# Output projection of a two-layer mixer: the place of the fourth products, one written order for two blocks, and two gate weights

## The chip, the cores and the metric

The kernel runs on one core of a Trainium2 chip. A core has a matrix engine (TensorE, PE in the profile, with its weight loads as PEld), a vector engine (DVE), a scalar engine (ACT), a general engine (GpSimd, POOL) and a queue for transfers (SyncE, SP). Matmuls write into banks of PSUM, 128 x 512 fp32 each; DVE and ACT read them from there. Operands lie in SBUF. The metric is the device time of one execution in microseconds; lower is better.

## The reference

Two layers over 1024 latent tokens and 256 context tokens, model width 1024. The even layer has a convolution branch and a recurrent branch, each with a SiLU gate, then one output projection. The odd layer is a multi-scale pooling mixer. Cut to what this change touches:

```python
# even layer: the recurrent branch's gate
y_b = y_b * silu(gb)                     # gb = h @ w_in[:, last quarter]
out = concat([y_a, y_b]) @ w_out
# odd layer
z = h @ p["w_in"]                        # 1024 -> 4096
u, g = split(z)                          # 2048 each
y = einsum(multiscale_pool(u), w_grp) * scale
out = (y * silu(g)) @ p["w_out"]         # 2048 -> 1024
x = x + gate * out
return rmsnorm(x, final_g)
```

The change lies in the product with the odd layer's `w_out` (the output projection below), and, in its last part, in the gate `silu(gb)` of the even layer.

## The kernel before, in words

Everything is kept transposed: a tile has 128 channels as partitions and the 1024 tokens along the free axis, in two halves of 512. Every fp32 factor is split into a high part (a cast to fp32r on ACT) and a low part (a subtraction on DVE or POOL), and each matmul runs as three: high by high, high by low, low by high.

**The output projection.** The contraction over 2048 channels is done in two halves of 1024: part 0 (tiles 0 to 7 of y) and part 1 (tiles 8 to 15). Part 0's result is scaled by the gate, added to the residual and written back to memory; part 1 adds to that and goes on to the final norm. Each part runs over four blocks, m = 0, 2, 4, 6, of two output tiles by two token halves. A block is a two by two matrix product in Winograd's form with seven block products in place of eight. On the side of y the seven operands are called b11, t1, t2, b21, t3, b22, t4 (`BOPS`); on the side of the weights they are numbered: 1 goes with b11, 5 with t1, 6 with t2, 2 with b21, 7 with t3, 3 with b22, 4 with t4. "The fourth product" is that of weight 4 and t4. `prod` (line 1148) issues one of them: four k steps of three matmuls into one bank.

A block uses three PSUM banks out of a pool of four: qa takes b11 and, after ACT has copied it to qb, b21; qc takes t1 and b22; qb, which starts from the copy, takes t2, t3 and t4. After a product has finished an output quarter, or half of it, `put` takes it out. In part 0 the half results of t1 and t2 are copied by ACT (`keep_part`, line 1205, tiles s_wo), because their banks are filled again; that of t3 is copied too (`copied`, line 1826, tile b_wo). The finished quarter is then put into a residual tile xp by DVE (`gated`, line 1819), which SP has loaded from `x1_part` (line 1883) and stores back (line 1892). Two kinds of xp tiles take turns, so a load waits for the store of two uses before.

**Orders.** Most of the kernel is ordered by a scheduler that simulates it when the kernel is built; `tc.issue_after(i)` (and `held`) puts what is traced inside behind instruction i on i's engine. `linked` (line 1835) chains the products of part 0 on PE, so their order is the written one; in part 1 `quad` (line 1163) leaves the order to the scheduler. In part 0 the order of a block is b11, [t4 of the block before], t1, t2, b21, b22, t3 (in the first block t3 before b22); `quad_linked` returns the block's own t4 as a function `last`, which the next block calls as `pend`. The last one, t4 of block 6, is handed to the first block of part 1. From block 4 of part 1 on, `last_half0` does the first token half alone, and the rest is in a written order of its own.

**Weights.** `wo1_weights` loads two raw tiles for a block (`wr`, two buffers, line 1116), forms the sums and splits seven operands (`wquad_steps`, line 1112): weight 1, then the difference for 7, the sum for 5, and so on; 4 is the last. Seven tiles out of a ring of eight take the results, so a split can wait for a product of the block before.

**Operands of y.** The seven operands per part have been stored to memory (`y_raw`) and are loaded back by `y_operand` (line 1691), 512 KB at a time, two loads each, then split by ACT and DVE. With `later` the splits are put off. For t3, b22 and t4 of part 0 this happens after the last gate's SiLU; for part 1 in the `ahead` of its first block, t3 first, then b22 and t4, whose raw data is loaded into their own low tiles (no raw tile). `x2_load` (line 1910) loads two residual tiles for part 1.

**The gates of the recurrent branch** (lines 1217 to 1245). For j = 3 to 8 the loop takes, in a fixed order on each engine: the raw weight of product j + 2 (`gb_weights`: cast on ACT, subtraction on POOL, tiles wh_gb, wl_gb; from j = 6 on the first weights of the output projection, wh_wob, wl_wob), the two SiLUs of product j (`gb_silu`, tiles sb from a ring of four), the product j + 2 on PE, and then `gated(j - 1)`: load of a recurrent row yr, multiplication on DVE, cast on ACT (ybh), subtraction on POOL (ybl), with `fill` steps of the convolution on DVE in between. The product wob then reads ybh and ybl.

Of the kernel before, what the change touches and what calls it, by code (L numbers as in the profile page):

```python
# [16 lines left out]
S = 1024  # L17
# [3 lines left out]
KT = D // P  # L21
# [30 lines left out]
def body(ctx, tc, xT, ctxT, cc, ccol, modT, modW, win, gw, wout, wu, grp, wg, wo1, small, edge, ident, outT):  # L52
    nc = tc.nc
# [55 lines left out]
    class Written:  # L109

        def __init__(self, eng):
            self.eng, self.last = eng, None
# [1050 lines left out]
    def quad(w, name, ops, put, ahead=None, tied=False, mid=None, pend=None):  # L1163
        p1, p2, p3, p4, p5, p6, p7 = w
        a, c, b = psum(f"qa_{name}"), psum(f"qc_{name}"), psum(f"qb_{name}")
        if pend is None:
            prod(a, p1, ops["b11"], True, False)
        else:
            pend[0](a, p1, ops["b11"], True, False)
        with tc.high_priority(offset=EVAC):  # L1170
            evac = nc.scalar.copy(b, a)
        if pend is not None:
            pend[1]()
        if mid is not None:
            with tc.issue_after(evac.ins):
                mid()
        prod(c, p5, ops["t1"], True, False)
        with tc.high_priority(offset=EVAC):
            put(1, 1, c, 0)
        prod(b, p6, ops["t2"], False, False)  # L1180
        with tc.high_priority(offset=EVAC):
            put(0, 1, b, 0)
        prod(a, p2, ops["b21"], False, True)
        with tc.high_priority(offset=EVAC):
            put(0, 0, a, None)
        w = None
        if ahead is not None:
            with tc.issue_after(evac.ins):
                w = ahead()
        mm = prod(b, p7, ops["t3"], False, False)  # L1190
        with tc.high_priority(offset=EVAC):
            put(1, 1, b, 1)
        with tc.issue_after(mm.ins) if tied else nullcontext():
            prod(c, p3, ops["b22"], False, True)
        with tc.high_priority(offset=EVAC):
# [37 lines left out]
    gb_product(5, gws[5])  # L1233
    gated(1, 3)
    for j in range(3, KT + 1):
        if 3 < j < KT - 1:
            gb_weights(j + 2)
        if j < KT:
            gb_silu(j)
        if 3 < j < KT - 2:  # L1240
            gb_product(j + 2, gws[j + 2])
        gated(j - 1, (0, 0, 4, 5, 5, 3, 1, 0)[j - 1])
        if j == KT:
            gb_weights(KT + 1)
            fill(8)
        ln_sums()
# [444 lines left out]
    def y_operand(ops, part, name, raw_tile, alloc, later=None, hold=None):  # L1691
        hi, lo = [], []
        for q in range(2):
            if raw_tile is None:
                lo.append(alloc(f"y{part}_{name}l{q}", F32R))
                r = lo[q].bitcast(F32)
            else:
                r = raw_tile(f"yr_{part}_{name}_{q}")
            nc.sync.dma_start(r, y_raw[part][name][:, q * S : (q + 1) * S])
# [11 lines left out]
    yops = [{}, {}]  # L1711

    def y_operands(part, raws, names=BOPS, alloc=None, later=None, hold=None):
        for name in names:
# [19 lines left out]
    for m in range(0, NK, 2):  # L1734
# [63 lines left out]
        w = quad(wq, f"g{m}", bx, to_gate, first_out if m == NK - 2 else None)  # L1798
        if m == NK - 2:
            with tc.issue_after(silu[0].ins):  # L1800
                y_operands(0, iter([xtile] * 7), BOPS[4:])
        for i in range(2):
            for h in range(2):
                gt = rows(ys[m + i][:, HALF[h]])
# [30 lines left out]
    def linked(*args):  # L1835
        with held(chain[0]):
            chain[0] = prod(*args)

    def quad_linked(w, name, ops, put, ahead, order, pend):
        p1, p2, p3, p4, p5, p6, p7 = w  # L1840
        a, c, b = psum(f"qa_{name}"), psum(f"qc_{name}"), psum(f"qb_{name}")
        linked(a, p1, ops["b11"], True, False)
        with tc.high_priority(offset=EVAC):
            evac = nc.scalar.copy(b, a)
        if pend is not None:
            pend()
        linked(c, p5, ops["t1"], True, False)
        with tc.high_priority(offset=EVAC):
            put(1, 1, c, 0)
        linked(b, p6, ops["t2"], False, False)  # L1850
        with tc.high_priority(offset=EVAC):
            put(0, 1, b, 0)
        linked(a, p2, ops["b21"], False, True)
        with tc.high_priority(offset=EVAC):
            put(0, 0, a, None)
        with tc.issue_after(evac.ins):
            nxt_ = ahead()
        for name in order:
            if name == "t3":
                linked(b, p7, ops["t3"], False, False)  # L1860
                with tc.high_priority(offset=EVAC):
                    put(1, 1, b, 1)
            else:
                linked(c, p3, ops["b22"], False, True)
                with tc.high_priority(offset=EVAC):
                    put(0, 1, c, 1)

        def last():
            linked(b, p4, ops["t4"], False, True)
            with tc.high_priority(offset=EVAC):  # L1870
                put(1, 0, b, None)
        return nxt_, last

    last_ = None
    for m in range(0, KT, 2):

        def put(i, h, x, part, m=m, parts={}):
            if part == 0:
                keep_part(parts, f"wo0_{m}", i, x)
                return  # L1880
            xp_n[0] += 1
            t = (vtile, lambda name: atile(name)[:, :H])[xp_n[0] % 2](f"xp{m}_{i}_{h}")
            nc.sync.dma_start(t, x1_part[m + i][:, HALF[h]])
            if part == 1:

                if i == 1:
                    x = copied(f"wo0_{m}", x)
                s = x if i == 0 else parts[i]
                nc.vector.tensor_tensor(out=s, in0=x, in1=parts[i], op=add)
                x = s  # L1890
            gated(m + i, t, x)
            nc.sync.dma_start(x1_part[m + i][:, HALF[h]], t)
            if (m, i, h, part) == (2, 1, 1, 1):
                y_sums(NK - 2)
        def nxt(m=m):
            if m < KT - 2:
                with tc.issue_after(stored[0].ins):
                    return wo1_weights(0, m + 2)
            w = wo1_weights(1, 0)
            y_operands(1, iter([xtile]), BOPS[3:4])  # L1900
            return w

        if m == KT - 2:
            with tc.issue_after(loaded[0].ins):
                y_operands(1, iter([xtile] * 2), BOPS[1:3])
        w, last_ = quad_linked(w, f"wo0_{m}", yops[0], put, nxt, ("b22", "t3") if m else ("t3", "b22"), last_)
        if m == 2:
            with tc.issue_after(loaded[0].ins):
                y_operands(1, iter([xtile]), BOPS[:1], lambda name, dt: xtile(name, dt), hold=copied_[0])
# [4 lines left out]
                nc.sync.dma_start(x1[k], x1_part[k])  # L1914

    x2_load(0)
    for m in range(0, KT - 4, 2):
# [7 lines left out]
        def ahead():  # L1925
            if m == 0:
                y_operands(1, iter([xtile, None, None]), BOPS[4:])
            w = wo1_weights(1, m + 2)
            x2_load(m + 2)
            return w  # L1930

        w = quad(w, f"wo1_{m}", yops[1], put, ahead, pend=None if m else (linked, last_))


    ops = yops[1]
# [21 lines left out]
    def last_half0(m, w, ahead=None):  # L1957
# [3 lines left out]
        prod(a, p1, ops["b11"], True, False)  # L1961
        with tc.high_priority(offset=EVAC):
            evac = nc.scalar.copy(b, a)
        mm = prod(d, p4, ops["t4"], True, True)
        with tc.high_priority(offset=EVAC):
            gated(m + 1, y0, d)
        nxt = None
        if ahead is not None:
            with tc.issue_after(evac.ins):
# [16 lines left out]

    m = KT - 4
    wa = w
    wb, _, _ = last_half0(m, wa, ahead)
    _, tail["pe"], tail["dve"] = last_half0(m + 2, wb)  # L1990


# [218 lines left out]
```

## Time and profile before

| | |
|---|---|
| median of three runs | 1275.95 us (1275.37 to 1275.96) |
| the profiled execution's own time | 1272.99 us |
| its span | 1271.2 us, 16213 instructions |
| PE busy | 1252.5 us (99%), 5858 matmuls |
| PEld, DVE, ACT, POOL busy | 1034.5, 1141.8, 654.9, 291.8 us |
| mean granted TensorE clock | 0.996 |
| read, written | 137.18 MB, 44.04 MB, 143 GB/s over the span |
| gates of the recurrent branch | about 440 to 500 us |
| part 0 of the output projection | from 1093.7 us |
| part 1, first block | from about 1173 us |

A row of the time line has the start in us from the span's start, the duration in us, the engine, the line of the code, the operation, out<-in by tile names, the shapes, how many such instructions stand together, and in brackets how long the engine sat idle before it and what ended that. Matmuls overlap: each is shown with 0.39 us, and a new one starts every 0.23 us, so a stall of PE is longer than the idle time that the row shows. A row of waits has the waiting engine, tile and line, what it waited for, then us in total, how often, and the longest. A row of stretches gives the busy time of each engine in that stretch with the number of instructions.

### The profile page before, as it was taken

To read this page: it belongs to the slowest core of one execution; us is meant where nothing else is said; L and a number is where in the kernel's file an instruction comes from. 1 tells how busy PE (TensorE), PEld (TensorE's weight loads), DVE (VectorE), ACT (ScalarE), POOL (GpSimd) and SP (SyncE) were. 2 spreads that over 40 slices of the span, in tenths; PEclk is the share of its full clock that TensorE was granted. 3 is DMA by queue.
4 is the path that set the end of the run, shared out by engine and by line. 5 is a ranking of instruction groups with operands and counts; after the bars stand their busy time and mean duration, and the time that the engine had idled before them with its cause. 6 is when DMAs were issued, how large, how long until landed. Compare 5 with 4: busy or idle time off the path is not lost. (4 is left out here: it accounts for less than half of the span.)

```text
span 1271.2 us, 16213 instructions
## 1 busy us (share of the span) xinstructions
PE 1252.5 (99%) x5858; PEld 1034.5 (81%) x5858; DVE 1141.8 (90%) x1748; ACT 654.9 (52%) x955; POOL 291.8 (23%) x176
## 2 busy tenths in 40 slices
PE   9999999999999999999999999999999999999996
PEld 7788888888888887888887788788888888778785
DVE  7799999999999999988978979999999977877876
ACT  8464566556656533137435446644444344735542
POOL 0015364536453556433210022000000000000003
PEclk9999999999999999999999999999999999999998
DMA  9970111112111234442526665344432334868723
GB/s 378 387 251 28 58 59 67 42 53 64 62 63 59 77 114 133 158 140 84 172 91 226 207 216 160 105 151 141 135 122 83 125 116 156 299 198 271 283 69 133
DMA packets 78705, 182.29 MB, mean 143 GB/s; under 512 B 7712, under 2 KB 23328, under 8 KB 78624
## 3 DMA queue, kind: packets, MB, share of 16 engines
q1 hardware_dynamic: 69632, 176.53, 40.7%
q10 hardware_dynamic: 8992, 4.72, 1.3%
q8 instruction: 46, 0.75, 0.3%
q14 instruction: 35, 0.29, 0.1%
HBM read 137.18 MB, written 44.04 MB: 143 GB/s over the span
## 5 line engine op out<-in xcount | busy, mean ns | idle before, releaser
L670 DVE SCALAR_TENSOR_TENSOR conv<-u,sm,conv 128x505 f32<-128x505 f32 (+6 forms) x224 | 153.7, 744 | 1.0
L1943 POOL TENSOR_TENSOR o<-x,rr 128x256 f32<-128x256 f32 (+1 forms) x10 | 9.7, 1009 | 453.4 <-ACT rr L1943 453.4
L670 ACT ACTIVATE l<-g,sm 128x512 f32<-128x512 f32 (+1 forms) x96 | 58.7, 619 | 57.7 <-PE g L670 57.0
L670 POOL TENSOR_TENSOR l<-l,l 128x1280 f32<-128x1280 f32 x16 | 47.1, 2965 | 25.6 <-ACT l L670 15.1
L670 PE MATMUL wob<-ybl,wh_wob 128*128 128x512 f32 x128 | 49.9, 390 | 1.1 <-POOL ybl L670 1.1
L670 PE MATMUL va<-h0h,wl_va 128*128 128x512 f32 x128 | 49.9, 390 | 0.2 <-DVE wl_va L670 0.2
L670 PE MATMUL wob<-ybh,wl_wob 128*128 128x512 f32 x128 | 49.9, 390 | 0.1
L670 PE MATMUL gb<-h0l,wh_gb 128*128 128x512 f32 x128 | 49.8, 389 | 0.0
L670 PE MATMUL gb<-h0h,wh_gb 128*128 128x512 f32 x128 | 49.8, 389 | 0.0
L670 PE MATMUL va<-h0l,wh_va 128*128 128x512 f32 x128 | 49.8, 389 | 0.0
L670 PE MATMUL wob<-ybh,wh_wob 128*128 128x512 f32 x128 | 49.8, 389 | 0.0
L670 PE MATMUL va<-h0h,wh_va 128*128 128x512 f32 x128 | 49.8, 389 | 0.0
L670 PE MATMUL gb<-h0h,wl_gb 128*128 128x512 f32 x128 | 49.8, 389 | 0.0
L670 DVE TENSOR_TENSOR_SCAN l<-l,l 128x256 f32<-128x256 f32 (+1 forms) x32 | 48.7, 1522 | 1.1
L98 ACT CAST wq_wo<-wr_wo 128x512 fp32r<-128x512 f32 x48 | 28.9, 620 | 40.1 <-DMA wr_wo<-wo 17.8
L670 DVE SCALAR_TENSOR_TENSOR conv<-cL,wsum,conv 128x506 f32<-128x506 f32 (+3 forms) x70 | 48.1, 744 | 0.2
L670 POOL TENSOR_TENSOR l<-l,uc 128x1280 f32<-128x1280 f32 x16 | 47.7, 3005 | 0.0
L98 ACT CAST wq_g<-wr_g 128x512 fp32r<-128x512 f32 x48 | 28.3, 621 | 33.5 <-DVE wr_g L1133 12.6
L670 PE MATMUL xb<-h0l,wh_xb 128*128 128x512 f32 x112 | 43.8, 391 | 0.0
L670 PE MATMUL xb<-h0h,wh_xb 128*128 128x512 f32 x112 | 43.8, 391 | 0.0
L670 PE MATMUL xb<-h0h,wl_xb 128*128 128x512 f32 x112 | 43.6, 389 | 0.0
L670 PE MATMUL vg<-h0h,wh_vg 128*128 128x512 f32 x112 | 43.6, 389 | 0.0
(624 smaller groups left out, 4320.1 us busy)
## 6 DMA issues: line engine op xcount, KB each, us to landing
modw<-modW SPq DMA_DIRECT2D x16, 512.0 KB, 10.2
x_part<-xp SPq DMA_DIRECT2D x32, 256.0 KB, 2.9
mod<-modT SPq DMA_DIRECT2D x32, 256.0 KB, 3.5
wr_v<-wfold SPq DMA_DIRECT2D x16, 512.0 KB, 3.6
wr_g<-wg SPq DMA_DIRECT2D x16, 512.0 KB, 4.9
wr_wo<-wo SPq DMA_DIRECT2D x16, 512.0 KB, 4.6
mod<-modT SPq DMA_DIRECT2D x14, 512.0 KB, 4.5
yr_t<-y_t SPq DMA_DIRECT2D x14, 512.0 KB, 7.3
```

The lines of the kernel that those rows point to most:

```text
L98: return (nc.scalar.copy(hi, src), eng.tensor_tensor(out=lo, in0=src, in1=hi.bitcast(F32), op=sub))
L670: last[eng] = f(*args, **kw)
L1943: tail[eng] = f(*args, **kw)
```

## The change

Five edits. (1) In `quad`, the pending product comes after t1, not before; no caller hands it one any more after the change. (2) In the gate loop, `gb_weights(j + 2)` for j = 5 and 6 stands behind `gb_silu(j)`. (3) The splits of b22 and t4 of part 0 are put off until after the copy of the first block's t2 (`kept_`). (4) In `quad_linked`, `pend` comes after t1 and its put. (5) The first two blocks of part 1 are written out in one order with a small class, `Quad`, chained on PE; the loads of b22 come before those of t4, and x of block 2 behind t4's; block 2's own t4 runs in `last_half0` of block 4.

```diff
@@ quad
-        if pend is not None:
-            pend[1]()
...
-        prod(c, p5, ops["t1"], True, False)
+        if pend is None:
+            prod(c, p5, ops["t1"], True, False)
+        else:
+            pend[0](c, p5, ops["t1"], True, False)
+            pend[1]()
@@ gates
     for j in range(3, KT + 1):
-        if 3 < j < KT - 1:
+        if j == 4:
             gb_weights(j + 2)
         if j < KT:
             gb_silu(j)
+        if 4 < j < KT - 1:
+            gb_weights(j + 2)
@@ y_operand
-            nc.sync.dma_start(r, y_raw[part][name][:, q * S : (q + 1) * S])
+            d = nc.sync.dma_start(r, y_raw[part][name][:, q * S : (q + 1) * S])
+            if name in ("b22", "t4"):
+                y_loaded[name == "t4"] = d
@@ last gate block
             with tc.issue_after(silu[0].ins):
-                y_operands(0, iter([xtile] * 7), BOPS[4:])
+                y_operands(0, iter([xtile]), BOPS[4:5])
+                y_late = []
+                y_operands(0, iter([xtile] * 2), BOPS[5:], later=y_late)
@@ quad_linked
-        if pend is not None:
-            pend()
         linked(c, p5, ops["t1"], True, False)
         with tc.high_priority(offset=EVAC):
             put(1, 1, c, 0)
+        if pend is not None:
+            pend()
@@ part 0, weights of the next block
         def nxt(m=m):
+            if m == 0:
+                with tc.issue_after(kept_[0].ins):
+                    for v in y_late:
+                        split(*v, nc.vector)
@@ part 1, blocks 0 and 2
-        w = quad(w, f"wo1_{m}", yops[1], put, ahead, pend=None if m else (linked, last_))
...
+    class Quad:
...
+        def run(self, op):
+            n, p, first, last, args = dict(
+                b11=("a", 1, True, False, None), t1=("c", 5, True, False, (1, 1, 0)),
+                t2=("b", 6, False, False, (0, 1, 0)), b21=("a", 2, False, True, (0, 0, None)),
+                t3=("b", 7, False, False, (1, 1, 1)), b22=("c", 3, False, True, (0, 1, 1)),
+                t4=("b", 4, False, True, (1, 0, None)))[op]
+            linked(self.bank(n), self.w[p], yops[1][op], first, last)
+            if args is not None:
+                i, h, part = args
+                with tc.high_priority(offset=EVAC):
+                    self.put(i, h, self.bank(n), part)
...
+    q0.run("b11")
+    q0.copy()
+    q0.run("t1")
+    last_()
+    q0.run("t2")
+    q0.run("b21")
+    with tc.issue_after(q0.evac.ins):
+        late_ = []
+        y_operands(1, iter([None]), BOPS[5:6])
+        y_operands(1, iter([xtile]), BOPS[4:5])
+        with held(y_loaded[0]):
+            y_operands(1, iter([None]), BOPS[6:], later=late_)
+        w = wo1_weights(1, 2)
+        for v in late_:
+            split(*v, nc.vector)
+        with held(y_loaded[1]):
+            x2_load(2)
+    q2 = Quad(w, "wo1_2", wo1_put(2))
+    q2.run("b11")
+    q0.run("t3")
+    q0.run("b22")
+    q2.run("t1")
+    q2.copy()
+    q0.run("t4")
+    q2.run("t2")
+    q2.run("b21")
+    with tc.issue_after(q2.evac.ins):
+        w = wo1_weights(1, 4)
+        x2_load(4)
+    q2.run("b22")
+    q2.run("t3")
@@ last_half0 (block 4 of part 1)
-        mm = prod(d, p4, ops["t4"], True, True)
+        if pend is None:
+            mm = prod(d, p4, ops["t4"], True, True)
+        else:
+            mm = linked(d, p4, ops["t4"], True, True)
...
+        if pend is not None:
+            pend("t4")
```

More of the change, by code (lines that the diff above doesn't have):

```diff
@@ L1837, in linked @@
             chain[0] = prod(*args)
+        return chain[0]
     def quad_linked(w, name, ops, put, ahead, order, pend):
@@ L1916, in body, with wo1_put @@
     x2_load(0)
-    for m in range(0, KT - 4, 2):
+    def wo1_put(m):
         def put(i, h, x, part):
@@ L1924, in put, with __init__, bank, copy @@
                 square_fin(m + i, h, slice(0, H), v)
[L1925 to L1930, printed above, removed]
-        w = quad(w, f"wo1_{m}", yops[1], put, ahead, pend=None if m else (linked, last_))
+        return put
+    class Quad:
+        def __init__(self, w, name, put):
+            self.w, self.name, self.put = dict(zip(range(1, 8), w)), name, put
+            self.ps = {}
+        def bank(self, n):
+            if n not in self.ps:
+                self.ps[n] = psum(f"q{n}_{self.name}")
+            return self.ps[n]
+        def run(self, op):
[9 more added lines that the diff above has]
+                    self.put(i, h, self.bank(n), part)
+        def copy(self):
+            with tc.high_priority(offset=EVAC):
+                self.evac = nc.scalar.copy(self.bank("b"), self.bank("a"))
@@ new lines, in body @@
+    q0 = Quad(w, "wo1_0", wo1_put(0))
+    for n in "acb":
+        q0.bank(n)
+    q0.run("b11")
[15 more added lines that the diff above has]
+            x2_load(2)
@@ L1955, in fin_add, with last_half0 @@
         return nc.vector.tensor_tensor(out=acc_, in0=acc_, in1=q, op=add)
-    def last_half0(m, w, ahead=None):
+    def last_half0(m, w, ahead=None, pend=None):
         p1, p2, p3, p4, p5, p6, p7 = w
@@ L1960, in last_half0 @@
         (x0, x1_), (y0, y1) = [[x1[m + i][:, h] for h in HALF] for i in range(2)]
-        prod(a, p1, ops["b11"], True, False)
+        with held(chain[0] if pend is not None else None):
+            prod(a, p1, ops["b11"], True, False)
         with tc.high_priority(offset=EVAC):
             evac = nc.scalar.copy(b, a)
-        mm = prod(d, p4, ops["t4"], True, True)
+        if pend is None:
+            mm = prod(d, p4, ops["t4"], True, True)
+        else:
+            mm = linked(d, p4, ops["t4"], True, True)
         with tc.high_priority(offset=EVAC):
             gated(m + 1, y0, d)
+        if pend is not None:
+            pend("t4")
         nxt = None
@@ L1988, in body, with last_weights @@
     wa = w
-    wb, _, _ = last_half0(m, wa, ahead)
+    def last_weights():
+        w = wo1_weights(1, KT - 2)
+        x2_load(KT - 2)
+        return w
+    wb, _, _ = last_half0(m, wa, last_weights, q2.run)
     _, tail["pe"], tail["dve"] = last_half0(m + 2, wb)
```

2 lines of the change are left out of this document (1 added, 1 removed).

## The prediction

> **What bounds the kernel now.** I read the page first, then the stretches of 40 us of the output projection, then the waits of TensorE.
>
> ```profile
> 1100.00:1140.00 40.00, 37.92 (x166) 30.76 (x165) 31.89 (x46) 20.08 (x32) 0.00 (x0) 1.00 0.67 220
> 1140.00:1180.00 40.00, 38.72 (x169) 31.14 (x168) 32.65 (x47) 19.57 (x31) 0.00 (x0) 1.00 0.82 278
> 1180.00:1220.00 40.00, 38.84 (x169) 31.40 (x169) 31.64 (x45) 22.65 (x35) 0.00 (x0) 1.00 0.57 202
> ```
>
> ```profile
> PE qb_wo L1152 <- ACT b_wo L1828: 2.2, 2, 1.3
> PE qb_wo L1152 <- ACT s_wo L1207: 1.2, 1, 1.2
> ```
>
> The columns of the stretches are busy us of PE, PEld, DVE, ACT and POOL, then granted clock, DMA share and GB/s. PE is busy for 115.5 of the 120 us, at clock 1.00: this stage is bound by the matmuls, and all that any new order can win is the 4.5 us between them and a little at their restarts. These two rows head the waits of PE in the whole kernel: it waits for ACT to copy a bank (b_wo, s_wo).
>
> **Unit of the sums.** Twelve matmuls make a product, and the starts below give their pitch (1108.95 to 1109.18): 0.23 us, so a product is 2.72 us. I call the pairs of column tiles block 0, 2, 4, 6, and write t4(2) for the product on operand t4 of block 2. A stall is start minus previous start minus 0.23, and each restart loses 0.11 more on its second matmul (1108.61 to 1108.95).
>
> **Part 1: two operands of the first half are split later.** PE stops at t3(0):
>
> ```profile
> 1107.04 0.39 PE L1155 MATMUL qa_wo<-y_b21h,wq_wo 128*128 128x512 f32 x1
> 1108.61 0.50 PE L1152 MATMUL qb_wo<-y_t3h,wq_wo 128*128 128x512 f32 x1 [1.19 <-ACT s_wo L1207]
> 1108.95 0.39 PE L1154 MATMUL qb_wo<-y_t3l,wq_wo 128*128 128x512 f32 x1
> 1109.18 0.39 PE L1155 MATMUL qb_wo<-y_t3h,wq_wo 128*128 128x512 f32 x1
> ```
>
> ```profile
> 1106.08 1.05 ACT L98 CAST y_t4h<-yr_t 128x1024 fp32r<-128x1024 f32 x1 [1.75 <-DMA yr_t<-y_t]
> 1107.03 1.04 ACT L98 CAST y_b22h<-yr_b 128x1024 fp32r<-128x1024 f32 x1
> 1107.98 0.58 ACT L1207 COPY s_wo<-qb_wo 128x512 f32<-128x512 f32 x1
> ```
>
> The bank qb is full after t2(0), but its copy s_wo stands on ACT behind a cast of t4 that waits for its DMA, and behind a cast of b22. The change puts the four casts of b22 and t4 behind that copy; they run on ACT and DVE while t3(0) runs (2.72 us; the first b22 cast and its subtraction take 1.05 and 1.22). No load is added, and none moves. Worth: 1.34 + 0.11 = **1.45 us**. If that cover is gone, b22(0) waits instead, at most the 1.45 again.
>
> **Part 2: t4 of a block runs after the next block's b11 and t1**, no longer between them. The two stalls meant are these:
>
> ```profile
> 1135.72 0.39 PE L1155 MATMUL qa_wo<-y_b11h,wq_wo 128*128 128x512 f32 x1
> 1137.01 0.50 PE L1152 MATMUL qb_wo<-y_t4h,wq_wo 128*128 128x512 f32 x1 [0.90 <-ACT b_wo L1828]
> ...
> 1175.55 0.39 PE L1155 MATMUL qa_wo<-y_b11h,wq_wo 128*128 128x512 f32 x1
> 1177.21 0.50 PE L1152 MATMUL qb_wo<-y_t4h,wq_wo 128*128 128x512 f32 x1 [1.27 <-ACT b_wo L1828]
> ```
>
> They cost 1.06 + 0.11 and 1.43 + 0.11. A product more in between covers both. But t1 now comes 2.72 us earlier, and what it needs is late too: its weight (fifth of seven, split on ACT and DVE after the block's second raw tile has landed) and its bank qc, which the block before gives back when DVE has put it into the residual. The rows for blocks 2, 4 and 6:
>
> ```profile
> 1117.85 0.74 DVE L1820 SCALAR_TENSOR_TENSOR xp<-qc_wo,m,xp 128x512 f32<-128x512 f32 x1
> ...
> 1138.80 0.68 DVE L99 TENSOR_TENSOR wq_wo<-wr_wo,wq_wo 128x512 fp32r<-128x512 f32 x1
> ...
> 1158.51 0.74 DVE L1820 SCALAR_TENSOR_TENSOR xp<-qc_wo,m,xp 128x512 f32<-128x512 f32 x1
> ...
> 1159.31 0.19 PEld L1152 LDWEIGHTS qc_wo<-y_t1h,wq_wo 128*128 128x128 f32 x1 [0.42 <-DVE xp L1820]
> ```
>
> Without any stall t3(0) starts at 1107.27, and t1(2), t1(4), t1(6) follow after 3, 10 and 17 products: at 1115.4, 1134.5 and 1153.5. By the rows of before, bank or weight stand ready at 1118.6, 1139.0 (the low half, which the third matmul reads, ends at 1139.5) and 1159.3. The lateness is 3.2, 4.6 and 5.8 us; a wait at an earlier one covers the later, so the largest counts: w is between 0 and 5.8 if nothing is ready later than before. What makes them ready follows PE's events in part (the bank is full 1.45 earlier after part 1; the second raw tile is loaded when the block before has split its last weight, which waits for t2), and in part the DMAs. I take the middle, w = 2.9. Before, t1(6) starts at 1159.31 with t4(4) done; after, at 1153.5 + w with t4(4) still to come, so the same work is reached at 1156.2 + w: -3.1 + 2.9 = **-0.2 us** for part 1 and the blocks 2 to 6 of part 2 together (their stalls at 1108.61 and 1137.01 are in it). The stall at 1177.21 comes on top, with t1 of the second half's block 0 (weights and x tiles without a write-back) in no such need: **-1.5 us**.
>
> The wait that is added lies with the loads, too: the t4 evacuation is every fourth use of the xp tiles, and each xp load waits for the store of two uses before; t4's store is now 2.72 later, and SP's queue (weight loads among it) stands behind.
>
> ```profile
> wr_wo<-wo SPq DMA_DIRECT2D x11, 512.0 KB, 5.7
> ```
>
> The raw weights take 5.7 us at the median of this stage. [...]
>
> **Part 3: second half, blocks 0 and 2 in one written order.** Before, SP has the second load of b22 behind two loads of x, which wait for tiles that the split of t3 gives back:
>
> ```profile
> 1182.44 0.54 SPq L1699 DMA_DIRECT2D y_b22l<-y_b  x1
> 1190.25 2.11 SPq L1914 DMA_DIRECT2D x<-x_part  x2
> 1192.41 0.42 SPq L1699 DMA_DIRECT2D y_b22l<-y_b  x1
> ```
>
> ```profile
> 1193.62 0.39 PE L1155 MATMUL qb_wo<-y_t3h,wq_wo 128*128 128x512 f32 x1
> 1194.66 0.50 PE L1152 MATMUL qc_wo<-y_b22h,wq_wo 128*128 128x512 f32 x1 [0.65 <-ACT y_b22h L98]
> 1195.67 0.50 PE L1152 MATMUL qb_wo<-y_t2h,wq_wo 128*128 128x512 f32 x1 [0.51 <-ACT qb_wo L1171]
> ```
>
> PE loses 0.81 + 0.78 + 0.11 there. After, b22's loads come first, x after t4's, and every bank rests two products (5.4 us) between its uses. I take all of it: **-1.7 us**; bounds 0 to -1.8. The x loads now stand behind t4's; block 2 first needs them after nine products, 24.5 us after the half's start (1173.1, one product before the end of 1175.55 + 0.23). Issued as now, until 1192.4, they have 5 us to land; if that cover goes, evacuations wait, and PE only after the two products of rest.
>
> **Part 4: two gate weights behind their gates.** PE waits at the stage after the recurrence for POOL's low half of the last rows:
>
> ```profile
> 494.96 0.50 PE L670 MATMUL wob<-ybl,wh_wob 128*128 128x512 f32 x1 [1.11 <-POOL ybl L670]
> ```
>
> ```profile
> 473.00 1.30 POOL L670 TENSOR_TENSOR ybl<-sb,ybh 128x512 fp32r<-128x512 f32 x1 [3.04 <-ACT ybh L670]
> 474.27 2.41 POOL L670 TENSOR_TENSOR wl_gb<-wr_gb,wh_gb 128x1024 fp32r<-128x1024 f32 x1
> ...
> 484.29 2.40 POOL L670 TENSOR_TENSOR wl_wob<-wr_wob,wh_wob 128x1024 fp32r<-128x1024 f32 x1
> ```
>
> ```profile
> 475.44 2.39 DVE L670 TENSOR_TENSOR lnsum<-lnsum,u 128x512 f32<-128x512 f32 x2
> ...
> 485.63 1.60 DVE L670 TENSOR_TENSOR sb<-yr,sb 128x512 f32<-128x512 f32 x1
> ```
>
> ```profile
> 492.00 0.60 ACT L670 ACTIVATE sb<-gb 128x512 f32<-128x512 f32 x1 [0.91 <-POOL ybl L670]
> ```
>
> All four engines have a fixed order here. The two DVE rows are long because POOL's subtraction of a weight runs: lnsum ends 0.55 after 476.68, and so with the other (usual is 0.68). A gate's second SiLU waits for POOL's ybl (the last row), so the cast behind it comes 2.1 us later than before and POOL's weight starts at about 476.0 and 487.2 instead of 474.27 and 484.29. At the first place DVE meets it between two sums and comes out 1.1 later; at the second its multiply is already through and 0.9 is won back. Net at ybl: **+0.3**, bounds -0.9 and +1.5.
>
> **Sum.** -0.2 - 1.5 - 1.7 + 0.3 = -3.1 us. The profiled execution took 1272.99 us (its span 1271.2), 2.96 under the median 1275.95 of the three runs; -3.1 on that median is 1272.8.
>
> **The rivals.** (A) *The same waits at another product*: the t1 products find bank and weight no earlier than before, w = 5.8 or a little over: -0.2 in all, 1275.8. For it: the row at 1159.31 already waits for the bank. Against: three of the releases follow PE.
> (B) *Slower: the write-back ring.* From t4's end to the bank's return the round behind block 4 took 19.4 us (t4(2) starts at 1137.01 and takes 2.83; the put into the residual ends at 1159.25), and the new order leaves five products, 13.6 us, to the next t1 of that bank. If that round keeps its length, t1(6) is late by 5.8, and if the other two (to t1(4) and to t1 of the next half) and t1(2) are late by half as much, 2.9, 2.9 and 1.6, the waits are 13.2 in all in place of 2.9, the sum is +7.2 and the time 1283.2. It decides from waits of 8.6 in all. Against: ACT, DVE and SP's queue serve raw weights in the same round, so part of its length is queueing that a new order may lose.
> (C) *The written order starves block 2*: if SP sends its raw weights behind the loads of y that now come first, by one landing (5.7 us) more than they have to spare, b11(2) of the second half stops for that: +2.6, 1278.6, slower by a hair. Before, SP did send them first, though they are traced behind y.
> (D) No effect of the first half's t4 move alone, if the scheduler moves DVE's order with it: w = 0, -6.0, 1270.0.
>
> **How the numbers follow.** Two executions of this kernel differ by up to 0.6 us, and 0.2% (2.6 us) is what I call a change. Likeliest, with D in it: 0.47, its own range 1269.5 to 1273.4. A: 0.24. B: 0.20. C: 0.09. So faster 0.47, same 0.24, slower 0.29. The range goes from w = 0 with a gain in part 4 (1269.0) to where B has four fifths of its lateness (1280.5).
>
> **What would show it.** Part 1: s_wo ahead of the casts of b22, no stall at t3(0). Part 2: no PE wait for b_wo; at t1 of blocks 2, 4, 6 waits for xp or for a weight, 2.9 in sum (over 6: A; over 9: B). Part 3: both b22 loads ahead of x, no wait in the first two blocks. Part 4: POOL's two weights at 476 and 487, the stall at ybl 1.3 to 2. A span above 1273.8 makes the forecast wrong.

## The result, and the profile after

The changed kernel takes 1276.75 us (median of 22 runs, 1274.08 to 1278.48), the kernel before beside it 1274.81 us (22 runs, 1272.85 to 1278.65). The ratio is 1.0015, with a 95% interval of 1.0008 to 1.0022: about 1.9 us slower, where 3.1 us faster was forecast. The profiled execution has a span of 1273.5 us (before 1271.2). The 1275.95 from which the forecast counted was the median of three runs, 1.1 us above that of 22.

All stalls of PE, added up as in the prediction (start minus previous start minus 0.23, where that is over 0.03), by stage and kernel, in us:

| stage | before | after |
|---|---|---|
| start, to 60 us | 2.86 | 3.55 |
| gates, 440 to 520 | 1.76 | 0.72 |
| 660 to 820 | 2.84 | 2.87 |
| part 0 of the output projection, to 1172, and t4(6) | 4.65 | 6.51 |
| part 1, blocks 0 and 2, 1182 to 1202 | 1.86 | 2.43 |
| tail, from 1222 | 2.41 | 2.42 |
| 60 to 140 and 820 to 960 | 0.87 | 0.88 |
| whole span | 17.26 | 19.38 |

The start is not touched by the change and lies between 2.8 and 3.9 in the profiles of this study, so the 0.7 there is chance. The rest: the gates win 1.0, part 0 loses 1.9, part 1 loses 0.6.

PE's waits in the changed kernel, in the same columns as before (waiter, releaser, us, times, longest):

```profile
PE qc_wo L1152 <- DVE xp L1828: 2.8, 2, 1.8
PE qa_wo L1155 <- DVE wq_wo L99: 1.9, 2, 1.2
```

The waits for ACT's copies s_wo and b_wo are gone, as meant. In their place PE waits for the bank qc and for a low half of weights. The time line of PE shows where:

```profile
1114.46 0.50 PE L1155 MATMUL qa_wo<-y_b11h,wq_wo 128*128 128x512 f32 x1 [1.25 <-DVE wq_wo L99]
1118.88 0.47 PE L1152 MATMUL qc_wo<-y_t1h,wq_wo 128*128 128x512 f32 x1 [1.82 <-DVE xp L1828]
...
1120.33 0.63 PE L1155 MATMUL qc_wo<-y_t1h,wq_wo 128*128 128x512 f32 x1
1120.76 0.63 PE L1152 MATMUL qc_wo<-y_t1h,wq_wo 128*128 128x512 f32 x1
...
1122.89 0.63 PE L1155 MATMUL qc_wo<-y_t1h,wq_wo 128*128 128x512 f32 x1
...
1159.91 0.47 PE L1152 MATMUL qc_wo<-y_t1h,wq_wo 128*128 128x512 f32 x1 [0.95 <-DVE xp L1828]
```

b11(2) stops for 1.42 us, t1(2) for 1.99, t1(6) for 1.11 (each by the formula above, a little more than the idle time in the bracket). Between 1120.33 and 1122.89 the matmuls come every 0.43 us in place of 0.23, with no wait shown. The stretches of the same kernel say why (busy us of PE, PEld, DVE, ACT, POOL, then granted clock, DMA share, GB/s):

```profile
1116.60:1120.01 3.41, 1.59 (x7) 0.85 (x7) 3.41 (x7) 1.71 (x3) 0.00 (x0) 1.00 0.33 124
1120.01:1123.42 3.41, 3.41 (x10) 2.63 (x9) 1.22 (x2) 0.00 (x0) 0.00 (x0) 0.50 0.58 183
1123.42:1126.84 3.42, 3.42 (x17) 2.83 (x16) 1.23 (x2) 1.11 (x2) 0.00 (x0) 1.00 0.25 30
```

For 3.41 us TensorE ran at half clock (0.50), which costs 1.7 us. The pause ahead of it lies in the stretch before.

In part 1 both loads of b22 now go out ahead of x of block 2, but each of t3's raw tiles (yr_t) goes out behind one of t4's:

```profile
1179.40 0.72 SPq L1703 DMA_DIRECT2D y_b22l<-y_b  x1
1180.16 0.90 SPq L1703 DMA_DIRECT2D y_t4l<-y_t  x1
1182.31 0.32 SPq L1703 DMA_DIRECT2D yr_t<-y_t  x1
1183.51 0.32 SPq L1703 DMA_DIRECT2D y_t4l<-y_t  x1
1184.47 0.32 SPq L1703 DMA_DIRECT2D yr_t<-y_t  x1
```

Before, both of t3's loads were issued from 1178.18 on (row yr_t x2). On ACT the second cast of b22 waits for its data ahead of the casts of block 2's first weights, and b11 of block 2 waits for these, as PE's rows under ACT's show:

```profile
1188.87 1.05 ACT L98 CAST y_b22h<-y_b22l 128x1024 fp32r<-128x1024 f32 x1 [4.30 <-DMA y_b22l<-y_b]
1189.83 1.13 ACT L98 CAST wq_wo<-wr_wo 128x512 fp32r<-128x512 f32 x2
```

PE, same kernel:

```profile
1190.49 0.50 PE L1152 MATMUL qa_wo<-y_b11h,wq_wo 128*128 128x512 f32 x1 [0.38 <-ACT wq_wo L98]
1191.84 0.50 PE L1155 MATMUL qa_wo<-y_b11h,wq_wo 128*128 128x512 f32 x1 [0.61 <-DVE wq_wo L99]
```

These stops of b11(2), 1.52 us with their restarts, come with the later fourth products and not with the written order, as `e3` and `e6` below show.

In the gates POOL's two weights start at 476.90 and 486.02, and no matmul of wob waits any more; one product gb waits 0.60 us for the first of them.

### The profile page after: what moved, and what is told of

Its sections match the earlier page's. It is cut to its first block, busy times and chain, and to the rows that moved or that the text cites. A ratio compares the mean times of both kernels' runs of the same rounds, so it can differ in the third digit from the quotient of the medians.

```text
span 1273.5 us, 16213 instructions
## 1 busy us (share of the span) xinstructions
PE 1254.7 (99%) x5858; PEld 1036.0 (81%) x5858; DVE 1139.2 (89%) x1748; ACT 655.9 (51%) x955; POOL 295.0 (23%) x176
## 5 line engine op out<-in xcount | busy, mean ns | idle before, releaser
L670 PE MATMUL vg<-h0l,wh_vg 128*128 128x512 f32 x112 | 43.6, 389 | 0.0
```

Source lines behind the costliest of these rows:

```text
L670: last[eng] = f(*args, **kw)
```

## The experiments

Every ratio is against the kernel before, run on the same chip beside it, with its 95% interval.

### Each part of the change alone

`e1_gates` has the gate loop's hunk, `e2_splits` the late splits, `e3_t4` the later fourth products, `e4_order` the written order of part 1 (with `last_` before t1, as before). The core of each:

```diff
# e1
-        if 3 < j < KT - 1:
+        if j == 4:
             gb_weights(j + 2)
...
+        if 4 < j < KT - 1:
+            gb_weights(j + 2)
# e2
-                y_operands(0, iter([xtile] * 7), BOPS[4:])
+                y_operands(0, iter([xtile]), BOPS[4:5])
+                y_late = []
+                y_operands(0, iter([xtile] * 2), BOPS[5:], later=y_late)
# e3, in quad_linked, and the like in quad
-        if pend is not None:
-            pend()
         linked(c, p5, ops["t1"], True, False)
...
+        if pend is not None:
+            pend()
# e4
-        w = quad(w, f"wo1_{m}", yops[1], put, ahead, pend=None if m else (linked, last_))
+    q0 = Quad(w, "wo1_0", wo1_put(0))
...
+    q0.copy()
+    last_()
+    q0.run("t1")
```

> The kernel before with the gate weights' new place alone. Theory from the trace after: the stall of wob for ybl goes (1.38 and 0.39 us) and one of 0.4 for the gate weight comes, so about 1.1 us faster than before (ratio 0.9991). The prediction: +0.3 us, a stall of 1.3 to 2 for ybl stays.

> The kernel before with the late splits of b22 and t4 alone. Theory: the stall at t3(0) goes (-1.45 us), but weight 1 of block 2 stands on ACT and DVE behind the four splits, so b11(2) waits about 1.5 us: 0 in all. Rival (the prediction): -1.45 us and no new wait. A third: b11(2) waits longer than t3(0) did, slower by up to 1 us.

> The kernel before with the later place of the fourth products alone (first half, and the first block of the second). [...] Rival B: the write-back ring is slower, t1 waits of over 9 us in sum, +7. The prediction's middle: -0.2 - 1.5 without part 1's 1.45, about -0.3.

> The kernel before with the written order of the first two blocks of the second half alone, t4 of the last block of the first half before t1 as before. Theory from the trace after: waits of b11 of block 2 for its weights (0.65 and 0.89 us) and of t3 (0.48 and 0.42) in place of 1.87: +0.6 us. Rival (the prediction): -1.7 us with no wait. Rival C: one landing later, +2.6.

| kernel | median us | ratio | interval |
|---|---|---|---|
| e1, gates | 1274.52 | 1.0000 | 0.9991 to 1.0009 |
| e2, late splits | 1270.73 | 0.9965 | 0.9953 to 0.9978 |
| e3, t4 later | 1276.01 | 1.0009 | 1.0000 to 1.0017 |
| e4, written order | 1281.34 | 1.0053 | 1.0039 to 1.0067 |
| before | 1274.62 | | |

The theories for `e2` and `e4` missed by far; `e3` is 0.09% slower, about 1.2 us, where the prediction's middle was 0.3 us faster. The late splits win 0.35%, three times what their stall is worth; the written order loses 0.53%; the gates alone can't be told from no change, and their forecast of 0.9991 stands at the edge of the interval. The sum of the four is +0.27%, the whole change +0.15%, so the parts do not simply add.

In `e2` the stall at t3(0) is gone and b11(2) stops for 1.43 in its place, as the theory had it. PE's row on the time line of `e2`:

```profile
1115.17 0.50 PE L1155 MATMUL qa_wo<-y_b11h,wq_wo 128*128 128x512 f32 x1 [1.27 <-DVE wq_wo L99]
```

DVE's rows ahead of it in the same kernel:

```profile
1112.68 0.69 DVE L1132 TENSOR_TENSOR ws_wo<-wr_wo,wr_wo 128x512 f32<-128x512 f32 x1 [1.44 <-DMA wr_wo<-wo]
1113.30 1.22 DVE L99 TENSOR_TENSOR y_t4l<-yr_t,y_t4h 128x1024 fp32r<-128x1024 f32 x1
1114.43 0.69 DVE L99 TENSOR_TENSOR wq_wo<-wr_wo,wq_wo 128x512 fp32r<-128x512 f32 x1
```

Weight 1 of block 2 stands behind a moved subtraction of t4. What `e2` wins lies later: at t4(2) (1.16 before, 0; but t1(4) and the start of part 0 lose 0.97 more), at t4(6) (1.54 before, 0) and in blocks 0 and 2 of part 1 (1.86 before, 0.23). Nothing of that is in the edit. Its SP queue tells a good part of it. In the kernel before, the raw weights of block 6 were sent at 1145.49, behind the load of a residual tile:

```profile
1145.08 0.32 SPq L1883 DMA_DIRECT2D xp<-x_part  x1
1145.49 0.86 SPq L1116 DMA_DIRECT2D wr_wo<-wo  x2
```

In `e2` they go ahead of it, 3.3 us earlier:

```profile
1142.18 2.07 SPq L1116 DMA_DIRECT2D wr_wo<-wo  x2
1144.30 0.42 SPq L1885 DMA_DIRECT2D xp<-x_part  x1
```

The scheduler, with the splits later, had exchanged the two.

In `e3` the two products t1 wait for the bank, 1.83 and 2.04 us, at 1119.79 and 1160.23: 1.4 us more than the waits for b_wo had cost (1.06 and 1.43), at another product. And b11(2) of part 1 stops, 1.08 us with its restarts, though `e3` has no written order. On ACT a cast of t4 that waits for its data stands ahead of the weights' casts:

```profile
1188.11 1.05 ACT L98 CAST y_t4h<-y_t4l 128x1024 fp32r<-128x1024 f32 x1 [7.97 <-DMA y_t4l<-y_t]
1189.07 1.13 ACT L98 CAST wq_wo<-wr_wo 128x512 fp32r<-128x512 f32 x2
```

PE in `e3`:

```profile
1191.68 0.50 PE L1155 MATMUL qa_wo<-y_b11h,wq_wo 128*128 128x512 f32 x1 [0.69 <-DVE wq_wo L99]
```

This product stops in all five profiled kernels with the later fourth products (the changed one, `e3`, `e6`, `e8`, `e12`: 1.1 to 2.4 us) and in none of the nine others, `e4`, `e5` and `e11` with the written order among them. How the later fourth product brings it about was not tested.

In `e4` t3 of block 0 stops for 1.62 and then 3.68 us, and the clock is halved from 1196.76 to 1203.59. PE on its time line:

```profile
1195.56 0.50 PE L1152 MATMUL qb_wo<-y_t3h,wq_wo 128*128 128x512 f32 x1 [1.46 <-ACT y_t3h L98]
1199.47 0.79 PE L1154 MATMUL qb_wo<-y_t3l,wq_wo 128*128 128x512 f32 x1 [3.41 <-DVE y_t3l L99]
```

DVE on the time line of `e4`, up to the subtraction that the second of these waits for:

```profile
1194.72 1.22 DVE L99 TENSOR_TENSOR y_t4l<-y_t4l,y_t4h 128x1024 fp32r<-128x1024 f32 x1
1195.85 0.68 DVE L1141 TENSOR_TENSOR wr_wo<-wr_wo 128x512 f32<-128x512 f32 x1
1196.46 1.22 DVE L99 TENSOR_TENSOR y_t4l<-y_t4l,y_t4h 128x1024 fp32r<-128x1024 f32 x1
1197.59 0.68 DVE L99 TENSOR_TENSOR wq_wo<-ws_wo,wq_wo 128x512 fp32r<-128x512 f32 x1
1198.19 1.22 DVE L99 TENSOR_TENSOR y_t3l<-yr_t,y_t3h 128x1024 fp32r<-128x1024 f32 x1
```

DVE does two subtractions of t4, which is due a product and more later, and two weight operations before t3's second.

### The change less one part

```diff
# e5: the changed kernel with
-        linked(c, p5, ops["t1"], True, False)
...
         if pend is not None:
             pend()
+        linked(c, p5, ops["t1"], True, False)
...
-    q0.run("t1")
     last_()
+    q0.run("t1")
# e6: the changed kernel without Quad; part 1 as before, t4(6) after t1 by quad's pend
```

> The changed kernel with the fourth products back ahead of t1 in the first half and in block 0 of the second; late splits, written order and gate weights stay. Theory 1, the parts interact: the waits for bank qc (1.99 and 1.11 us) and the half clock behind the first (1.7) go, the waits for b_wo (about 1.2 and 1.5) come back: some 2 us under the changed kernel, about 0.9985 of the kernel before. Theory 2, the parts add up: -3.9 (late splits alone) + 6.7 (written order alone) + 0 = +2.8, 1.0022.

> The changed kernel with the second half as before (t4 of the last block after t1 of its first block); late splits, later fourth products and gate weights stay. Theory 1, the parts interact: b11(2) waits 1.5 and t1(2) 2.0 for bank qc within 5 us of each other, the clock is halved for 3.4 us in some executions: the first half gives back what the late splits win, and only the 0.6 of the written order goes: 1.0005 to 1.001. Theory 2, the parts add up: -3.9 + 1.2 + 0 = -2.7, 0.998.

`e5` took 1275.08 us, 1.0011 (1.0002 to 1.0021), and `e6` 1275.28 us, 1.0010 (1.0001 to 1.0019). For `e6` theory 1 holds. For `e5` neither does, theory 2's 1.0022 by a hair: part 0 is as good as in `e2`, but t3 of block 0 stops for 1.08 and 3.56 us as in `e4`. With the late splits and the gates alone at 0.9964 (`e10` below), the later fourth products take back 0.46%, the written order takes back 0.47%, and both together 0.51%, by the intervals no more than one of them. So each of the two alone uses up what the late splits win.

### SP's queue: one load behind two others

```diff
# e9: the kernel before; e12: the changed kernel; in put of part 0
-            nc.sync.dma_start(t, x1_part[m + i][:, HALF[h]])
+            with held(loaded[0] if (m, i, part) == (4, 1, 1) else None):
+                nc.sync.dma_start(t, x1_part[m + i][:, HALF[h]])
```

In both, every engine but SP has the order that it had without the tie.

> The kernel before with one tie: the load of the residual tile for t3 of block 4 in the first half goes behind the two raw weight loads of block 6. All engines but SP keep their order, and the splits stay where they were. Theory: what the late splits won beyond the 1.4 us that b11(2) took back came from this exchange on SP's queue, which sends block 6's raw weights 3.3 us earlier; so the stalls at t1(6) and t4(6) (0.3 and 1.5) go and those of the next half's first blocks shrink: 2 to 3.5 us under the kernel before, 0.9975. Rival: it came from the casts' and subtractions' new order on ACT and DVE: no change, 0.9995 to 1.0005.

> The changed kernel with the tie on SP's queue that puts the residual load for t3 of block 4 behind both raw weight loads of block 6; no other engine's order changes. Theory: the bank qc that t1(6) waits for comes back a fixed 6.8 us of DVE work after the second raw tile of block 6 lands; the tile is sent 1.5 to 2 us earlier, the bank comes back as much earlier and the wait at t1(6) (1.2 us) goes: 1.0005. Rival: the bank follows PE's own events or the write-back of the residual: the wait stays.

`e9` took 1272.5 us, 0.9985 (0.9975 to 0.9996): 2.1 us under the kernel before. The stalls at t1(6) and t4(6) are gone and block 0 and 2 of part 1 lose 0.79 in place of 1.86. The theory holds: one load tied behind two others, with the few exchanges on the same queue that follow from it, was worth more than the edit's own stall. By the medians it accounts for about half of what the late splits win; in the profiled executions PE's stalls from 1093 to 1202 us fall from 6.5 to 3.3 in `e9` and to 2.7 in `e2`. The rest is not traced to one cause.

`e12` took 1275.98 us, 1.0008 (0.9998 to 1.0019), and its t1(6) has no stall. The time against the changed kernel is not resolved, but the chain that ends the wait is. DVE's first operation on the second raw tile of block 6, and the one that gives the bank qc back, in the changed kernel:

```profile
1152.21 0.69 DVE L1132 TENSOR_TENSOR ws_wo<-wr_wo,wr_wo 128x512 f32<-128x512 f32 x1 [1.46 <-DMA wr_wo<-wo]
1159.02 0.75 DVE L1828 SCALAR_TENSOR_TENSOR xp<-qc_wo,m,xp 128x512 f32<-128x512 f32 x1
```

The same two in `e12`:

```profile
1151.20 0.69 DVE L1132 TENSOR_TENSOR ws_wo<-wr_wo,wr_wo 128x512 f32<-128x512 f32 x1 [0.33 <-DMA wr_wo<-wo]
1158.01 0.74 DVE L1828 SCALAR_TENSOR_TENSOR xp<-qc_wo,m,xp 128x512 f32<-128x512 f32 x1
```

The distance is 6.81 us in both. It is the same in the kernel before (1151.70 to 1158.51), in `e2` (1149.29 to 1156.10), `e3` (1152.53 to 1159.34) and `e6` (1154.94 to 1161.75), while b22(4), whose result it takes out, starts anywhere from 1148.02 to 1151.65. The other kernels have 6.80 or 6.81 too. So the bank comes back when DVE's list reaches it, and that list starts when the raw tile has landed (in `e5`, `e9` and `e11` DVE came to it later than that); how far PE is does not enter.

At t1(2), the longest of the waits, it is the same with the second raw tile of block 2. In the changed kernel:

```profile
1111.97 0.69 DVE L1132 TENSOR_TENSOR ws_wo<-wr_wo,wr_wo 128x512 f32<-128x512 f32 x1 [0.81 <-DMA wr_wo<-wo]
1117.99 0.75 DVE L1828 SCALAR_TENSOR_TENSOR xp<-qc_wo,m,xp 128x512 f32<-128x512 f32 x1
```

From one to the other it takes 6.01 or 6.02 us in the nine kernels with the late splits and 4.87 or 4.88 in the five without, where DVE comes to the first without a wait: the late splits put one subtraction of t4 in between. In the kernel before, the last one starts at 1117.85, so the bank comes back no earlier in the changed kernel, though PE has filled it 1.6 us earlier (b22(0) starts at 1109.83 in place of 1111.47).

### DVE's order

```diff
# e11: e5, and in the written order of part 1
+        t3_ = []
-        y_operands(1, iter([xtile]), BOPS[4:5])
+        y_operands(1, iter([xtile]), BOPS[4:5], later=t3_)
+        for v in t3_:
+            t3_split = split(*v, nc.vector)
...
         for v in late_:
-            split(*v, nc.vector)
+            with held(t3_split[0]), held(t3_split[1]):
+                split(*v, nc.vector)
# e7: e2, and in nxt of block 0 of part 0
-                    for v in y_late:
+                    for v in y_late[:3]:
                         split(*v, nc.vector)
...
-                    return wo1_weights(0, m + 2)
+                    return wo1_weights(0, m + 2, y_late[3:] if m == 0 else ())
# and in wquad_steps
         ops[1] = op(a11, 1)
+        for v in behind:
+            split_held(*v, nc.vector, parted[1])
```

> The changed kernel with the fourth products back ahead of t1, and in the written order of the second half the two splits of t4 behind the second split of t3, on ACT and on DVE. SP, PE and POOL keep their order. Theory: what the written order costs is the place of t3's second subtraction behind two of t4 and two operations of weights; its wait of 3.56 us in block 0 and the half clock after it (6.83 us long, some 2 us lost) go: 4 to 5 us under the same kernel without this, 0.997 of the kernel before. Rival: t3's raw data lands too late, the wait stays at 2 us or more: 1.0.

> The kernel before with the late splits alone, and the last subtraction of t4 (1.2 us on DVE) behind that of weight 1 of block 2. Theory: the wait of b11(2) falls from 1.4 to about 0.3 us and nothing takes its place: 1.1 us under the late splits alone, 0.996. Rival: the bank qc is the later one, t1(2) waits for it instead, and the time is that of the late splits alone, 0.9965 to 0.997.

`e11` took 1271.21 us, 0.9973 (0.9963 to 0.9984), by the ratios 4.8 us less than `e5`: its t3 stops once, for 1.32 us, and the half clock of `e5` there is gone (the mean granted clock of the profiled execution is 0.997, against 0.994 in `e5`). The place of two splits was the price of the written order, not the written order itself. The edit moves casts on ACT and subtractions on DVE together, so it does not say which of them counts more; in `e5` the long stop ends with the subtraction of t3.

`e7` took 1270.43 us, 0.9968 (0.9957 to 0.9979), no different from `e2`. The rival holds for the time: b11(2) stops for 0.34 in place of 1.43, but t1(2) now for 0.43 (the bank) and t4(2) for 0.84 (ACT's copy b_wo). DVE has no gap from 1113.21 to 1124 in this kernel; a piece of its work taken from one product's way stands in another's.

### The clock

```diff
# e8: the changed kernel, before t1 of block 2 in part 0
+        if name == "wo0_2":
+            spare = pc.tile([P, H], F32, tag="c0", name="spare")
+            for k in range(3):
+                hi, lo = p1[:, k * P : (k + 1) * P], p1[:, H + k * P : H + (k + 1) * P]
...
         linked(c, p5, ops["t1"], True, False)
```

> The changed kernel with nine matmuls into a spare bank between b11 and t1 of block 2; all other engines keep their order. Their results are not used. Theory: the slow pitch of 0.43 us behind the wait for bank qc is the clock, halved for one window of 3.4 us after a window with 2 us of idling; nine matmuls take 2.05 us in place of that idling, the clock stays full, and the profiled span is 1.6 us shorter than that of the changed kernel; the median falls by less (0.5 to 1.2), since the window stands differently in each execution. Rival: the slow pitch has another cause (a busy memory port or late weight loads): t1(2) stays at 0.43 and the time goes up by 0 to 0.7.

`e8` took 1275.68 us, 1.0012 (1.0003 to 1.0021). With the pause filled the clock is 1.00 and the matmuls keep their pitch (16 of them in a stretch, against 10 at half clock in the changed kernel), as the stretches of `e8` show:

```profile
1116.60:1120.01 3.41, 3.41 (x16) 2.72 (x15) 3.41 (x6) 2.14 (x4) 0.00 (x0) 1.00 0.21 77
1120.01:1123.42 3.41, 3.41 (x16) 2.64 (x15) 2.08 (x4) 0.62 (x3) 0.00 (x0) 1.00 0.63 191
```

In steps of 3.413 us, the spacing measured in the clock records of two other executions (see the last section), two bounds of `e8` are 1117.46 and 1120.88, an estimate. The pause, which would have run from about 1117.7 to 1119.7, would by that again have lain between two bounds. So the slow pitch was the clock, not a busy port or late weights. The theory's time did not come, though: the span is 1273.5 again. From 1112 to 1132 PE lost 1.77 us beside the 2.05 of the nine matmuls, against 5.28 in the changed kernel, so 1.46 us were won there; t1(6) took back 0.9 of them (2.11 against 1.19 lost), since its bank does not follow PE, and the gate stage, which this edit does not touch, lost 1.88 in place of 0.72 in this execution. The medians of the two kernels are not told apart by their intervals.

### The best of it

```diff
# e10: the hunks of e1 and e2 together
```

> The late splits and the gate weights' new place, nothing else of the change. Theory: the gains add up; the gate stage loses 1.2 us on the mean of five profiled kernels with the new place and 1.7 on that of five without, so 0.5 us under the late splits alone, 0.996. Rival: the gate weights shift when the later stages meet the DMAs, and take back as much: 0.9965 to 0.9975.

`e10` took 1270.58 us, 0.9964 (0.9951 to 0.9976). It is faster than both kernels, and by these intervals not to be told from the late splits alone: whether the gates add the half microsecond stays open in the times. In the traces their stage loses 1.11 us on the mean of eight kernels with the new place (0.61 to 1.88) and 1.75 on that of six without (1.46 to 1.93).

## Why the prediction was wrong, point by point

Between the forecast of -3.1 us and the +2.1 of PE's stalls in the profiled pair lie 5.2 us: w in part 2 came 3.5 us too long, part 3 2.3 worse and part 4 1.3 better than forecast, and 0.7 is the untouched start.

**Part 1 (forecast -1.45).** The stall at t3(0) was sized right and went. Two sentences failed. "If that cover is gone, b22(0) waits" looked only at what uses the moved splits, not at what queues behind them on DVE: weight 1 of block 2, at b11(2), for 1.53 us with its restart. And "no load is added, and none moves" was wrong: the scheduler places loads by when it believes tiles to be free, and it moved them. In `e2` that was a gift; in the changed kernel the tile that mattered went out only later (1147.37, after a residual load at 1146.96).

**Part 2 (w = 2.9, between 0 and 5.8).** The waits at t1(2), t1(4) and t1(6) alone are 3.3 us in sum, but w as the prediction defined it, the start of t1(6) less 1153.5, came to 6.4. The upper bound was the right value, and a little short. The step that failed is "what makes them ready follows PE's events in part": `e12`, the 6.81 us at t1(6) and the 6.02 at t1(2) show that the bank follows DVE's list behind a landing. The rest of w is the 1.53 us at b11(2) and the clock. The -1.5 at 1177.21 came as forecast (t4(6) does not stop), but b11(2) of the second half, which no term of the sum had, stops for 1.52 in its place. The row at 1159.31, which the prediction had quoted for rival A, was the better witness, since PE already waited there for the bank, without any part of the change.

**The clock** was in no term. At its place it cost 1.7 us of the 6.4, after a pause that the change made. Since t1(6) has to wait for a landing, part of that would have been waited for there: in `e8`, 0.9 of the 1.46 us won.

**Part 3 (forecast -1.7).** Both b22 loads came early as foreseen, and the stalls at b22 and t2 (0.81 and 0.89) went. But the moved step was costed by the two products it helps. t3, whose loads had gone out together ahead of t4's second, now has each of them behind one of t4's, and its splits came behind those of t4 (`e4`, `e5`; `e11` puts that right): +6.7 alone. In the changed kernel blocks 0 and 2 lose 0.6 more than before, but of the stops there only the 0.9 at t3 are the written order's; the 1.5 at b11(2) are part 2's.

**Part 4 (forecast +0.3).** The sign failed: -1.0 in the profiled pair, just past the bound of -0.9, and about -0.6 on the means above. POOL's weights came at 476.90 and 486.02 where 476.0 and 487.2 were forecast. The second was earlier than forecast, and ybl was ready. In `e1`, `e6`, `e8` and `e10` wob stops all the same, for 0.8 to 0.9 us, for the low half of its own weight (at 502); why in these and not in the others is open.

**The rivals.** A was nearest in its mechanism: the bank comes no earlier (1117.99 against 1117.85, 1159.02 against 1158.51), as `e12` explains. Against its -0.2 the profiled pair shows +2.1 in stalls: part 3 cost 2.3 more than A counts for it, w was 0.6 over A's 5.8, the start 0.7, and part 4 won 1.3 more. B's ring did not decide: 3.3 us of waits at t1, not 13. C's +2.6 is nearest in size to the +1.9 of the medians, by luck: it had the place (b11 of block 2 in part 1) and not the reason, since the weights' casts stood on ACT behind one that waited for b22, and that product stops with the later fourth products even without the written order (`e3`, `e6`).

**The noise.** "Two executions of this kernel differ by up to 0.6 us" came from three runs; 22 runs of it spread over 5.8 us. So a span above 1273.8 was too loose a sign: the profiled span of the slower kernel is 1273.5.

## What to carry to other kernels

Before a wait is moved, find what its releaser stands behind: if that is an in-order list that starts with a DMA's landing, moving the waiting product moves the wait and need not shorten it. Whenever a scheduler places the queues, compare every queue's order after an edit, the DMA queue first; here an exchange of loads that nobody wrote was worth some 2 us, and two splits in the wrong place nearly 5. Try the parts of a change one by one: the best part of this one (0.35%) was hidden by two others that each took all of it back.

## What the hardware showed that was not expected

After a pause of 2 us (1.99 and 2.01) the clock was halved in two profiled executions, but not after every such pause. The clock record of the changed kernel begins at 7.27 us with full clock; the clock is half from 1120.01 to 1123.42 and full again until 1263.37. These stretches are 326, 1 and 41 times 3.413 us long; in the kernel before, the one of full clock from 5.33 to 1261.44 is 368 times 3.413. Cut into steps of that length, the pauses at t1 are as follows. In `after` and `e6` the steps are counted from the halving; in `e3`, `e8` and `e12`, whose clock does not change there, the place of the steps is an estimate.

| kernel | pause | in the first step, in the second | clock after |
|---|---|---|---|
| after | 1.99 | 1.99, 0 | half for 3.41 us |
| e6 | 2.01 | 2.01, 0 | half for 3.41 us |
| e12 | 1.99 | 0.76, 1.23 | full |
| e3 | 2.04 | 0.98, 1.06 | full |
| e8, t1(6) | 2.04 | 0.25, 1.79 | full |
| e6, t1(6) | 2.82 | 1.34, 1.48 | full |

The stretches of these steps in `e6`:

```profile
1116.79:1120.20 3.41, 1.57 (x8) 0.84 (x6) 3.41 (x7) 1.93 (x4) 0.00 (x0) 1.00 0.20 77
1120.20:1123.61 3.41, 3.41 (x9) 2.76 (x9) 1.78 (x3) 0.00 (x0) 0.00 (x0) 0.50 0.65 217
```

And in `e12`:

```profile
1115.61:1119.03 3.42, 2.60 (x10) 1.80 (x10) 3.42 (x7) 1.17 (x2) 0.00 (x0) 1.00 0.10 37
1119.03:1122.44 3.41, 2.18 (x9) 1.72 (x10) 3.38 (x6) 1.16 (x3) 0.00 (x0) 1.00 0.51 181
```

In the first two rows the pause lies in one step, which had PE busy for 1.59 and 1.57 of its 3.41 us, and the clock of the next step was 0.50. In the other rows it lies in two. There a step with 1.62 us busy (1158.42 to 1161.83 in `e8`, with 1.79 us of the pause) was followed by a clock of 1.00. What the clock goes by is not shown by these runs. The steps do not stand at the same place in every profiled execution (a step begins at 1120.01 in the changed kernel, at 1120.20 in `e6`). The same pause of 1.99 us cost 2 us at its place in `e12` and, with the half clock behind it, 3.7 in the changed kernel. The runs that were only timed list a mean granted clock, and it fits that this is part of why the changed kernel's runs lie 4.4 us apart. In the profiles the half clock at the span's end takes 9.7 us (before) and 10.2 (changed kernel), which alone makes a mean of 0.996; by these figures a mean of 0.994 takes some 14 us or more at half clock, about a halved step more, an estimate. Ten of the changed kernel's 22 runs list 0.994 and took 1277.4 us on average, six list 0.996 or 0.997 and took 1275.6; of the eleven runs of `e8` none lists 0.994. Which step was halved in a timed run is not on record.
